# Order of the input projection's units, rotation angles computed directly, and channels stored by one operation in a hybrid S5 and attention trunk on one core

## The chip, the cores and the metric

The kernel runs on one core of a Trainium2 chip. TensorE (PE) does the matmuls, VectorE (DVE), ScalarE (ACT) and GpSimd (POOL) the element work, SyncE (SP) issues most DMAs. The metric is the device time of one execution in microseconds; of several executions the median is given.

## What is computed

The reference is one inference step of a two-layer trunk (layer 0: S5 mixer and sliding-window attention side by side; layer 1: a convolution module; a ConvGLU after each) for two groups of requests with the same weights: a prompt of 16 + 1024 tokens and 8 sampled sequences of 8 tokens. The change lies in the first mixer:

```python
h = rmsnorm(x, p['g_mix'][layer])
z = h @ p['w_in_mix'][idx]                        # 1024 -> 512 + 512 + 128 + 128
u = z[..., :D_SSM]                                # S5 channels
q = z[..., D_SSM:D_SSM + D_Q]                     # 8 heads of 64
k = z[..., D_SSM + D_Q:D_SSM + D_Q + D_KV]
v = z[..., D_SSM + D_Q + D_KV:]
ya, sr, si = s5_mixer(u, ...)     # a = exp(lambda dt), h_t = a h_(t-1) + B u_t, y = C h + d u, gelu, half-GLU
yb, nk, nv = swa_prompt(q, k, v, rel_bias, sink, w_rows)     # 128-wide window, softmax with a sink
x = x + concatenate([ya, yb]) @ p['w_out_mix'][idx]
```

The S5 scan runs over blocks of eight tokens: eight steps inside a block are one matrix, and from block to block a state is turned by the angle of 8 steps and shrunk. For this the kernel needs cos and sin of theta times 8 a and theta times 128 b (a up to 15, b up to 8), theta being the angle of one step for each of 32 groups with 64 states: the rotation tables `ta` and `tb`, whose products make the table `T`.

## The kernel before

Tokens are split into two streams, A with 528 columns and B with 576; activations stand channel by token, and stream B also has the sampled tokens. Matrices are kept in two parts, a rounded high part and the rest, and each product of a weight piece and an activation takes three matmuls (high by high, high by low, low by high), each in two halves of columns. A `Unit` is one block of 128 output channels with its eight k steps of 128 inputs (four in the output projection of one mixer half). Its weights come in pieces of 128 x 512 (four k steps), loaded by SP into four buffers (`raw`), rounded by ACT into `whi` (L210) and completed by DVE into `wlo` (L216). `mm` (L295) does a unit's matmuls (L315), then its epilogue `epi_...` empties the sum: `take` (L530) multiplies by the normalization's factor (Rk) into `kT`, `vst`, `qst`, while `epi_u` (L1403) stores the S5 channels `us` with eight operations, one for each of the eight places in a block of tokens, and sends them to DRAM (`uD`). Two units may run k step by k step together, as a `Pair`.

The units' list in `build` sets the order: before, (k, v) of A as a pair, q x 4, u x 4 of A, then u x 4, k, v, q x 4 of B, each named here as uA, uB and so on. Behind it follow the output projection's attention half on A (oA, six of its eight units), the gate of S5's A half (gluA), two more oA, and the S5 half on A (`yaA`), and so on.

Beside the units run generators in the background: after each k step `pump` (L325) advances every one by half its rate; a step issues a few operations on the engines. They are `take_x(B)` (x of stream B, its normalization), `rest`, the S5 preparation `s5_prep` (power tables, four pairs of tables: e, a table that makes psk, and f, a table of six operations that PE turns into psf, L843 to L848 and L879), S5's main loop (stage 1 is matmuls `xr`, `xi`, L923; stage 3 is `yps`, L965; eight pieces of each), attention on A in blocks (`attn_A`: scores L1232, `softmax_rows`, turn L1219, output L1246) and the gelus of S5's outputs (L1062). All of this is laid down at build time: each engine executes its own instructions in the order of their emission, and waits for other engines by semaphores. `s5_rot` (L697) builds the rotation tables on POOL with no step in between: some 130 operations on 128 x 16 raise a cosine and sine to the needed powers, some 50 more double them up to `ta` and `tb`, and then for each of four j six wide operations of 128 x 576 make the product table `tj`, which two DMAs send to DRAM (`tD`). The S5 loop starts (NU0) after eight u units.

## Time and profile before

| | us |
| --- | --- |
| median of 3 executions | 2436.97 |
| lowest, highest | 2433.14, 2439.76 |
| profiled execution | 2437.08 |
| span of the profile | 2435.3 |
| PE busy | 2339.9 (96%) |
| DVE busy | 1683.2 (69%) |
| ACT busy | 987.5 (41%) |
| POOL busy | 234.7 (10%) |

Busy times are over the whole span. In the page's 40 slices (61 us each) PE has 7, 6, 8, 9, 8 and 8 tenths in the first six, and 9 in all the others but the last, and POOL 5, 9, 4, 0 and 2 tenths in the first five: what is not PE at work stands in the first six slices, which are the loads and the input projection and the S5 and attention work beside it. The rows of the trace there are in the section behind the change.

### The profile page before, as it was taken

The page shows a single profiled execution, that of the slowest core. Times are in us where ns is not written, and L with a number is a line of the kernel's source. Part 1 is how long each engine was busy: PE and PEld are TensorE (multiplying, and loading weights), DVE is VectorE, ACT ScalarE, POOL GpSimd, SP SyncE. Part 2 cuts the span into 40 slices and gives each one's busy share as a digit, 9 for nine tenths or more (in the row PEclk, how much of TensorE's full clock was granted, in tenths as well). Part 3 has the DMA queues.
Part 4 walks back from the last instruction along what each step waited for, and adds up shares of the span by engine and source line. Part 5 has one row for each costly group of instructions (what it writes and reads, how often), then busy time and mean ns, then how long its engine had stood idle before and what let it go on. Part 6 is the DMA issues. An engine that isn't in the chain of part 4 may idle for free.

```text
span 2435.3 us, 46080 instructions
## 1 busy us (share of the span) xinstructions
PE 2339.9 (96%) x18180; PEld 2289.5 (94%) x18180; DVE 1683.2 (69%) x3135; ACT 987.5 (41%) x1890; POOL 234.7 (10%) x557
## 2 busy tenths in 40 slices
PE   7689889999999999999999999999999999999998
PEld 6577789889999999999999999999999999999998
DVE  6977666653778588888887568888888665444443
ACT  6233443553434343433326343343434534333343
POOL 5940200000000000100101000000000000000000
PEclk9889999998999999999999999999999999999999
DMA  7755744224333523223222432333332423222322
GB/s 207 227 143 159 221 137 151 76 68 116 88 95 92 165 65 101 83 79 87 79 82 84 122 126 75 102 88 98 89 97 83 130 75 113 79 87 77 89 83 69
DMA packets 459598, 260.86 MB, mean 107 GB/s; under 512 B 57451, under 2 KB 446727, under 8 KB 458198
## 3 DMA queue, kind: packets, MB, share of 16 engines
q1 hardware_dynamic: 456246, 253.08, 35.6%
q0 software_dynamic: 3136, 4.85, 0.7%
q8 instruction: 143, 2.34, 0.4%
q14 instruction: 73, 0.60, 0.1%
HBM read 225.59 MB, written 35.52 MB: 107 GB/s over the span
## 4 chain that ended last, share of the span: by engine, by line
PE 81%; DVE 7%; ACT 4%; DMA 2%; issue 2%; SPq 0%; POOL 0%; DVEq 0%; ACTq 0%; POOLq 0%
PE pu L315 78%; DVE wlo L216 1%; ACT whi L210 1%; PE tps L1219 1%; ACT P L1183 1%; PE sps L1232 1%; DVE mx L1176 0%; PE psum_s L367 0%; DMA m<-mD 0%; PE ops L1246 0%; DMA fstt<-in_state_ffn 0%; DMA raw<-in_w_out_mix 0%; ACT xB L1739 0%; DVE P L1236 0%; DMA xA<-xaD 0%
## 5 line engine op out<-in xcount | busy, mean ns | idle before, releaser
L216 DVE TENSOR_TENSOR wlo<-raw,whi 128x512 fp32r<-128x512 f32 x720 | 489.5, 683 | 516.5 <-ACT whi L210 512.1
L210 ACT CAST whi<-raw 128x512 fp32r<-128x512 f32 x720 | 434.5, 608 | 703.5 <-PE pu L315 640.3
L1674 DVE SCALAR_TENSOR_TENSOR xA<-gl,pt,xA 128x528 f32<-128x528 f32 x240 | 182.8, 763 | 3.8 <-ACT xA L1668 1.5
L1674 DVE SCALAR_TENSOR_TENSOR xB<-gl,pt,xB 128x512 f32<-128x512 f32 x240 | 179.0, 746 | 4.3 <-ACT xB L1668 2.9
L1493 ACT ACTIVATE cv<-cv 128x592 f32<-128x592 f32 (+2 forms) x88 | 58.9, 670 | 154.6 <-DVE cv L1492 154.5
L315 PE MATMUL pu<-a0h,whi 128*128 128x288 f32 (+3 forms) x428 | 92.2, 298 | 12.0 <-ACT G L1472 5.0
L1491 DVE SCALAR_TENSOR_TENSOR cv<-G,pt,cv 128x592 f32<-128x592 f32 (+2 forms) x88 | 70.1, 796 | 43.3 <-ACT cv L1490 42.4
L315 PE MATMUL pu<-a4h,whi 128*128 128x288 f32 (+3 forms) x420 | 89.2, 294 | 9.9 <-DVE xA L437 7.1
L315 PE MATMUL pu<-a1h,whi 128*128 128x288 f32 (+3 forms) x428 | 91.3, 295 | 0.0
L315 PE MATMUL pu<-a0l,whi 128*128 128x288 f32 (+3 forms) x428 | 90.4, 293 | 0.3 <-DVE a0l L218 0.3
L315 PE MATMUL pu<-a0h,wlo 128*128 128x288 f32 (+3 forms) x428 | 90.3, 293 | 0.0
L315 PE MATMUL pu<-a3h,whi 128*128 128x288 f32 (+3 forms) x428 | 90.3, 293 | 0.0
L315 PE MATMUL pu<-a2h,whi 128*128 128x288 f32 (+3 forms) x428 | 90.0, 292 | 0.0
L315 PE MATMUL pu<-a1h,wlo 128*128 128x288 f32 (+3 forms) x428 | 89.8, 292 | 0.0
L315 PE MATMUL pu<-a1l,whi 128*128 128x288 f32 (+3 forms) x428 | 89.5, 291 | 0.0
L315 PE MATMUL pu<-a2l,whi 128*128 128x288 f32 (+3 forms) x428 | 89.3, 290 | 0.0
L315 PE MATMUL pu<-a7h,whi 128*128 128x288 f32 (+3 forms) x420 | 89.2, 294 | 0.0
L315 PE MATMUL pu<-a2h,wlo 128*128 128x288 f32 (+3 forms) x428 | 89.1, 290 | 0.0
L315 PE MATMUL pu<-a3h,wlo 128*128 128x288 f32 (+3 forms) x428 | 88.9, 289 | 0.0
L315 PE MATMUL pu<-a5h,whi 128*128 128x288 f32 (+3 forms) x420 | 88.9, 293 | 0.0
L315 PE MATMUL pu<-a3l,whi 128*128 128x288 f32 (+3 forms) x428 | 88.9, 289 | 0.0
L315 PE MATMUL pu<-a6h,whi 128*128 128x288 f32 (+3 forms) x420 | 88.2, 292 | 0.0
(663 smaller groups left out, 6827.2 us busy)
## 6 DMA issues: line engine op xcount, KB each, us to landing
raw<-in_ffn_w_up SPq DMA_DIRECT2D x352, 256.0 KB, 2.9
raw<-in_ffn_w_down SPq DMA_DIRECT2D x128, 256.0 KB, 2.8
raw<-in_conv_w_pw SPq DMA_DIRECT2D x96, 256.0 KB, 2.7
raw<-in_ffn_w_down SPq DMA_DIRECT2D x64, 192.0 KB, 2.5
xbD<-xB SPq DMA_DIRECT2D x3, 2304.0 KB, 8.6
xB<-xbD SPq DMA_DIRECT2D x6, 1152.0 KB
raw<-in_w_in_mix SPq DMA_DIRECT2D x24, 256.0 KB, 4.3
xaD<-xA SPq DMA_DIRECT2D x2, 2112.0 KB
```

Of the source, the lines that this page charges most:

```text
L210: nc.scalar.copy(hi, src)
L216: nc.vector.tensor_tensor(lo, src, hi.bitcast(F32), op=OP.subtract)
L315: nc.tensor.matmul(ps[:, ch, :c], wt, xt[:, off + ch * c:off + (ch + 1) * c], start=(k == 0 and pi == 0), stop=(k == nk - 1 and pi == 2))
L1183: nc.scalar.activation(pt[:, h, :], pt[:, h, :], AF.Exp, bias=nm[:, h:h + 1], accum_out=sm[:, h:h + 1])
L1219: nc.tensor.transpose(v[:, h, :], pt[:, 4 * kv + h, ko:ko + m], self.ident[:nq, :nq])
L1232: nc.tensor.matmul(vs[kv][:, hh, :], q[hs, 2 * pr + hh, :], self.kT[hs, kc0:kc0 + nk], start=True, stop=True)
L1491: nc.vector.scalar_tensor_tensor(c, G[:, 1:1 + n], wc(1), c, op0=OP.mult, op1=OP.add)
L1493: self.chain(lambda: None, lambda: None, lambda: nc.scalar.activation(c, c, AF.Gelu_apprx_tanh))
L1674: V.scalar_tensor_tensor(acc, gl[:, i:i + npp], w(i), acc, op0=OP.mult, op1=OP.add)
```

## The change

The projection's units are put in another order: of A all (u0 and u1 as a pair, u2, u3, k, v, q x 4), then of B u x 4, and then k, v, q x 4. The rotation tables are computed directly: the angle of each multiple (its multipliers come with the mask as constants) is reduced to +-pi by POOL, and ACT takes its sine four times, in place of powers and doublings; the rotation is a background generator at rate 1, which waits 12 steps between the reduction and the sines, and then does the same wide operations, with a tile and a DMA for each of the two halves. The S5 channels are stored by one operation with a strided output and a DMA that reads the rows in reverse order. S5's main loop starts after six u units, its tables at rate 0.7, attention counts only the q of A, and the mask is loaded before x.

```diff
-NU0 = 8
+NU0 = 6
 WQ = 10
+WR = 12
 WA = 6
 WF2 = 8
 SP = 1
 K1 = 5
 K2 = 6
 VR = 3
-RP = 1.0
+RP = 0.7
...
+MAGIC = 12582912.0
+_C2 = math.floor((2 * math.pi - 6.28125) * 2 ** 21) / 2 ** 21
+TWOPI = (6.28125, _C2, 2 * math.pi - 6.28125 - _C2)
...
-        self.mask16 = pp.tile([P, 16], F32, name="mask16", tag="mask16")
+        mask = pp.tile([P, 41], F32, name="mask16", tag="mask16")
+        self.mask16, self.mult = mask[:, :16], mask[:, 16:]
+        nc.sync.dma_start(mask, a["c_mask16"])
...
-        nc.sync.dma_start(self.mask16, a["c_mask16"])
...
+        thh, thl = pl[:, 16, :], pl[:, 17, :]
+        V.tensor_scalar(thh, th, 12288.0, -12288.0, op0=OP.add, op1=OP.add)
+        V.tensor_tensor(thl, th, thh, op=OP.subtract)
...
-        def renorm(r, i):
-            G.tensor_tensor(q1, r, r, op=OP.mult)
-            G.tensor_tensor(q2, i, i, op=OP.mult)
-            G.tensor_tensor(q1, q1, q2, op=OP.add)
-            G.tensor_scalar(q1, q1, -0.5, 1.5, op0=OP.mult, op1=OP.add)
-            G.tensor_tensor(r, r, q1, op=OP.mult)
-            G.tensor_tensor(i, i, q1, op=OP.mult)
-
-        def square(dr, di, r, i):
-            G.tensor_tensor(q1, r, r, op=OP.mult)
-            G.tensor_tensor(q2, i, i, op=OP.mult)
-            G.tensor_tensor(q1, q1, q2, op=OP.subtract)
-            G.tensor_tensor(q2, r, i, op=OP.mult)
-            G.tensor_copy(dr, q1)
-            G.tensor_scalar(di, q2, 2.0, None, op0=OP.mult)
-            renorm(dr, di)
-
-        G.tensor_copy(e[:, 0, 0, :], cs)
-        G.tensor_copy(e[:, 0, 1, :], sn)
-        renorm(e[:, 0, 0, :], e[:, 0, 1, :])
-        for _ in range(3):
-            square(e[:, 0, 0, :], e[:, 0, 1, :], e[:, 0, 0, :], e[:, 0, 1, :])
-        for i in range(1, 8):
-            square(e[:, i, 0, :], e[:, i, 1, :], e[:, i - 1, 0, :], e[:, i - 1, 1, :])
-        w1 = tz[:, 0:256].rearrange("p (a b) -> p a b", a=16)
-        w2 = tz[:, 256:512].rearrange("p (a b) -> p a b", a=16)
         ta = pp.tile([P, 2, 16, 16], F32, name="ta", tag="ta")
         tb = pp.tile([P, 2, 16, 9], F32, name="tb", tag="tb")
-        for tt, base in ((ta, 0), (tb, 4)):
-            G.memset(tt[:, 0, :, 0:1], 1.0)
-            G.memset(tt[:, 1, :, 0:1], 0.0)
-            n = 1
-            lvl = 0
-            while n < tt.shape[3]:
-                m = min(n, tt.shape[3] - n)
-                bc = lambda ri: e[:, base + lvl, ri, :].unsqueeze(2).to_broadcast([P, 16, m])
-                self.cmul(G, tt[:, 0, :, n:n + m], tt[:, 1, :, n:n + m], tt[:, 0, :, 0:m], tt[:, 1, :, 0:m],
-                          bc(0), bc(1), w1[:, :, :m], w2[:, :, :m])
-                n += m
-                lvl += 1
+        sines = []
+        for tt, mult, off, m in ((ta, self.mult[:, 0:16], 0, 256), (tb, self.mult[:, 16:25], 512, 144)):
+            n = tt.shape[3]
+            x, h, k, w = (tz[:, off + m * i:off + m * i + m].rearrange("p (g a) -> p g a", g=16) for i in range(4))
+            mb = mult.unsqueeze(1).to_broadcast([P, 16, n])
+            th = lambda i: self.pl[:, i, :].unsqueeze(2).to_broadcast([P, 16, n])
+            G.tensor_tensor(k, th(4), mb, op=OP.mult)
+            G.tensor_scalar(k, k, 1.0 / (2 * math.pi), MAGIC, op0=OP.mult, op1=OP.add)
+            G.tensor_scalar(k, k, MAGIC, None, op0=OP.subtract)
+            G.tensor_tensor(x, th(16), mb, op=OP.mult)
+            for c in TWOPI[:2]:
+                G.tensor_scalar(h, k, -c, None, op0=OP.mult)
+                G.tensor_tensor(x, x, h, op=OP.add)
+            G.tensor_tensor(w, th(17), mb, op=OP.mult)
+            G.tensor_scalar(h, k, -TWOPI[2], None, op0=OP.mult)
+            G.tensor_tensor(w, w, h, op=OP.add)
+            G.tensor_tensor(x, x, w, op=OP.add)
+            G.tensor_scalar(x, x, 3.1415925, -3.1415925, op0=OP.min, op1=OP.max)
+            G.tensor_scalar(h, x, 0.0, -2.0, op0=OP.min, op1=OP.mult)
+            G.tensor_tensor(h, h, x, op=OP.add)
+            G.tensor_scalar(h, h, -1.0, math.pi / 2, op0=OP.mult, op1=OP.add)
+            sines += [(tt[:, 0], h), (tt[:, 1], x)]
+        for _ in range(WR):
+            yield
+        for out, x in sines:
+            nc.scalar.activation(out, x, AF.Sin)
         for j in range(4):
             g4 = slice(4 * j, 4 * j + 4)
-            tt = pp.tile([P, 2, 4, 9, 16], F32, name="tj", tag="tj")
             t1 = tz[:, 0:576].rearrange("p (g q b) -> p g q b", g=4, q=9)
             t2 = tz[:, 576:1152].rearrange("p (g q b) -> p g q b", g=4, q=9)
             f1 = lambda ri: ta[:, ri, g4, :].unsqueeze(2).to_broadcast([P, 4, 9, 16])
             f2 = lambda ri: tb[:, ri, g4, :].unsqueeze(3).to_broadcast([P, 4, 9, 16])
-            self.cmul(G, tt[:, 0], tt[:, 1], f1(0), f1(1), f2(0), f2(1), t1, t2)
             for ri in range(2):
-                nc.gpsimd.dma_start(self.dq(self.tD, ri, j, 132),
-                                    tt[:, ri].rearrange("p g q b -> p g (q b)")[:, :, 0:132])
+                G.tensor_tensor(t1, f1(0), f2(ri), op=OP.mult)
+                G.tensor_tensor(t2, f1(1), f2(1 - ri), op=OP.mult)
+                tt = pp.tile([P, 4, 9, 16], F32, name="tj", tag=f"tj{ri}")
+                G.tensor_tensor(tt, t1, t2, op=OP.add if ri else OP.subtract)
+                G.dma_start(self.dq(self.tD, ri, j, 132), tt.rearrange("p g q b -> p g (q b)")[:, :, 0:132])
...
-        rel = SA[:, 0:392]
+        rel = self.sacc.rearrange("p a b c -> p (a b c)")[:, 0:392]
...
-            self.nq += 1
+            self.nq += s is self.A
...
-            src = ps[:, :, :s.c].rearrange("p a (k s) -> p a k s", s=8)
-            R = self.R0[s.name].rearrange("p (a k s) -> p a k s", a=2, s=8)
-            for t in range(8):
-                dst = us[:, 7 - t, :].rearrange("p (a k) -> p a k", a=2)
-                nc.vector.tensor_tensor(dst, src[:, :, :, t], R[:, :, :, t], op=OP.mult)
-            nc.sync.dma_start(dap(self.uD, j * P * 8 * NK + s.col0 // 8, [[8 * NK, P], [NK, 8], [1, kk]]), us)
+            nc.vector.tensor_tensor(us.rearrange("p s (a k) -> p a k s", a=2),
+                                    ps[:, :, :s.c].rearrange("p a (k s) -> p a k s", s=8),
+                                    self.R0[s.name].rearrange("p (a k s) -> p a k s", a=2, s=8), op=OP.mult)
+            nc.sync.dma_start(dap(self.uD, (j * P * 8 + 7) * NK + s.col0 // 8, [[8 * NK, P], [-NK, 8], [1, kk]]), us)
...
-                self.s5_rot()
+                self.add_bg(self.s5_rot(), 1)
...
-        def in_units(s, h):
+        hA, hB = (lambda: self.hx["A"]), (lambda: self.hx["B"])
+        def channels(s, h):
             us = [Unit(self.wblock(win, 0, KT, j * P), h, s, self.epi_u(s, j)) for j in range(4)]
-            ks = [Unit(self.wblock(win, 0, KT, 1024), h, s, self.epi_k(s)),
-                  Unit(self.wblock(win, 0, KT, 1152), h, s, self.epi_v(s))]
-            return us, ks + [Unit(self.wblock_q(j), h, s, self.epi_q(s, j)) for j in range(4)]
-        uA, kA = in_units(A, lambda: self.hx["A"])
-        uB, kB = in_units(B, lambda: self.hx["B"])
-        items += [Pair(kA[0], kA[1])] + kA[2:] + uA + uB + kB
+            return [Pair(us[0], us[1])] + us[2:] if s is A else us
+
+        def heads(s, h):
+            return [Unit(self.wblock(win, 0, KT, 1024), h, s, self.epi_k(s)),
+                    Unit(self.wblock(win, 0, KT, 1152), h, s, self.epi_v(s))] + [
+                        Unit(self.wblock_q(j), h, s, self.epi_q(s, j)) for j in range(4)]
+        items += channels(A, hA) + heads(A, hA) + channels(B, hB) + heads(B, hB)
```

Three places show how the operations stand. On ACT, behind the activations of stream B (y6h, y7h are their rounded parts), in front of S5's first tables; before:

```order
L813 COPY h_1069<-psh 128x256
L212 ACTIVATE y6h<-xB,pt 128x576
L212 ACTIVATE y7h<-xB,pt 128x576
L833 COPY bd<-bb 64x8x16 x2
L210 CAST whi<-raw 128x512
L833 COPY bd<-bb 64x8x16 x2
L210 CAST whi<-raw 128x512
```

and now:

```order
L217 ACTIVATE y7h<-xB,pt 128x576
L782 COPY a_871<-apw 128x32
L215 CAST whi<-raw 128x512 x2
L802 COPY h_957<-psh 128x256
L735 ACTIVATE ta<-tz 128x256 x2
L735 ACTIVATE tb<-tz 128x144 x2
L822 COPY bd<-bb 64x8x16 x2
```

The four sine operations stand in front of the first copies of bd, behind h; before there are none, and POOL had nothing to wait for there.

On DVE, around the last of the four f tables (ff, L843 to L848 before, L832 to L837 now). Before, it stands behind the first us of A:

```order
L216 TENSOR_TENSOR wlo<-raw,whi 128x512
L868 MEMSET kz 128x112
L871 SCALAR_TENSOR_TENSOR kz<-mask_115,pt,kz 128x16
L216 TENSOR_TENSOR wlo<-raw,whi 128x512
L1413 TENSOR_TENSOR us<-pu,Rk 128x66 x8
L843 TENSOR_TENSOR ff<-bb,apw 128x512
L844 TENSOR_TENSOR y_1552<-bb,apw 128x512
L845 TENSOR_TENSOR ff<-ff,y_1552 128x512
L846 TENSOR_TENSOR ff<-bb,apw 128x512
L847 TENSOR_TENSOR y_1552<-bb,apw 128x512
L848 TENSOR_TENSOR ff<-ff,y_1552 128x512
L216 TENSOR_TENSOR wlo<-raw,whi 128x512
```

and now behind the last q of A (L535 is `take`):

```order
L857 MEMSET kz 128x112
L860 SCALAR_TENSOR_TENSOR kz<-mask_115,pt,kz 128x16
L535 TENSOR_TENSOR qst<-pu,Rk 128x528
L221 TENSOR_TENSOR wlo<-raw,whi 128x512 x2
L535 TENSOR_TENSOR qst<-pu,Rk 128x528
L832 TENSOR_TENSOR ff<-bb,apw 128x512
L833 TENSOR_TENSOR y_1584<-bb,apw 128x512
L834 TENSOR_TENSOR ff<-ff,y_1584 128x512
L835 TENSOR_TENSOR ff<-bb,apw 128x512
L836 TENSOR_TENSOR y_1584<-bb,apw 128x512
L837 TENSOR_TENSOR ff<-ff,y_1584 128x512
L221 TENSOR_TENSOR wlo<-raw,whi 128x512
```

The last table stands behind ten units of the new order, where before it stood behind seven.

On PE, at the end of the projections (y7 is the last k step of the last unit, a4 the first of an output unit). Before:

```order
L315 MATMUL pu<-y7h,whi 128x288 x2
L315 MATMUL pu<-y7l,whi 128x288 x2
L315 MATMUL pu<-y7h,wlo 128x288 x2
L315 MATMUL pu<-a4h,whi 128x264 x2
L315 MATMUL pu<-a4l,whi 128x264 x2
L315 MATMUL pu<-a4h,wlo 128x264 x2
L923 MATMUL xr<-u,xf 64x138 x4
L923 MATMUL xi<-u,xf 64x138 x4
```

and now:

```order
L320 MATMUL pu<-y7h,whi 128x288 x2
L320 MATMUL pu<-y7l,whi 128x288 x2
L320 MATMUL pu<-y7h,wlo 128x288 x2
L1221 MATMUL sps<-kT,xB 128x256 x8
L1235 MATMUL ops<-xB,vA 64x512 x4
L1030 MATMUL sps<-ident,hs 128x128
L1031 MATMUL sps<-ident,hf 16x128
L1030 MATMUL sps<-ident,hs 128x128
L1031 MATMUL sps<-ident,hf 16x128
L1208 MATMUL tps<-ident,xA 128x128 x16
L1235 MATMUL ops<-xB,vA 64x512 x4
L320 MATMUL pu<-a4h,whi 128x264 x2
```

The scores of the last block (sps), the turns and outputs (tps, ops) and S5's last states (hs, hf) now stand between the last projection unit and the first output unit, where before nothing stood; S5's stage 1, which before stood after the first k step of the output unit, is gone from there.

## Rows read from the trace of the kernel before

**Rows 1.** Stretches: length; busy (count) of PE, PEld, DVE, ACT, POOL; clock; DMA; GB/s.

```profile
49.50:122.30 72.80, 49.12 (x373) 44.70 (x373) 70.06 (x124) 23.96 (x54) 67.71 (x119) 0.80 0.66 205
122.30:155.30 33.00, 28.56 (x182) 26.55 (x183) 21.61 (x56) 10.80 (x45) 23.77 (x21) 0.74 0.66 154
155.30:274.60 119.30, 108.33 (x818) 91.78 (x817) 87.54 (x231) 46.34 (x138) 15.58 (x22) 0.96 0.61 164
274.60:335.20 60.60, 49.53 (x382) 46.70 (x381) 37.42 (x77) 29.84 (x54) 18.81 (x33) 0.92 0.61 168
335.20:2435.30 2100.10, 2069.73 (x16203) 2049.04 (x16203) 1436.17 (x2541) 846.41 (x1532) 85.58 (x275) 0.99 0.32 95
```

**Rows 2.** Waits of PE, 49.5 to 274.6 us: total, times, longest.

```profile
PE psf L879 <- DVE xA L1236: 9.1, 1, 9.1
...
PE tps L1219 <- DVE xA L1192: 3.5, 3, 1.6
```

**Rows 3.** Timeline of DVE: start, duration, line, operation, shapes, idle before.

```profile
61.17 0.69 DVE L530 TENSOR_TENSOR qst<-pu,Rk 128x528 f32<-128x528 f32 x1
...
72.19 1.04 DVE L843 TENSOR_TENSOR ff<-bb,apw 128x512 f32<-128x512 f32 x1
...
77.53 0.78 DVE L823 TENSOR_TENSOR ee<-ct,apw 128x576 f32<-128x576 f32 x1
...
109.64 0.68 DVE L216 TENSOR_TENSOR wlo<-raw,whi 128x512 fp32r<-128x512 f32 x1
110.24 1.55 DVE L1413 TENSOR_TENSOR us<-pu,Rk 128x66 f32<-128x66 f32 x8
111.72 1.31 DVE L843 TENSOR_TENSOR ff<-bb,apw 128x512 f32<-128x512 f32 x1
...
122.27 1.64 DVE L216 TENSOR_TENSOR wlo<-raw,whi 128x512 fp32r<-128x512 f32 x1
```

**Rows 4.** Timeline of POOL: the rotation's operations.

```profile
90.76 0.40 POOL L589 TENSOR_TENSOR tz<-ta,e 128x128 f32<-128x128 f32 x1
...
111.00 1.16 POOL L588 TENSOR_TENSOR tz<-ta,tb 128x576 f32<-128x576 f32 x1
...
137.29 1.18 POOL L589 TENSOR_TENSOR tz<-ta,tb 128x576 f32<-128x576 f32 x1
```

**Rows 5.** Timeline of PE after the projections' end.

```profile
275.43 0.69 PE L923 MATMUL xr<-u,xf 128*64 128x138 f32 x8
...
278.07 1.10 PE L965 MATMUL yps<-u,m 128*128 128x138 f32 x8
...
288.51 0.48 PE L315 MATMUL pu<-a4h,whi 128*128 128x264 f32 x2 [3.87 <-DVE xA L437]
...
307.26 0.78 PE L315 MATMUL pu<-a4h,whi 128*128 128x264 f32 x2 [3.21 <-DVE xA L437]
```

**Rows 6.** Waits of PE, 274.6 to 335.2 us.

```profile
PE pu L315 <- DVE xA L437: 7.1, 2, 3.9
PE pu L315 <- ACT th L1421: 3.1, 3, 2.2
```

**Rows 7.** Timeline of DVE in one attention block.

```profile
222.94 1.29 DVE L1236 SCALAR_TENSOR_TENSOR xA<-sps,xB 128x512 f32<-128x512 f32 x2
224.26 2.29 DVE L1176 TENSOR_REDUCE mx<-xA 128x8 f32<-128x2048 f32 x1
...
245.14 2.19 DVE L1192 TENSOR_SCALAR xA<-xA,smx 128x256 f32<-128x256 f32 x8
```

**Rows 8.** Timeline of ACT in an attention block, and a table load.

```profile
226.78 0.51 ACT L1183 ACTIVATE xA<-xA,nm 128x256 f32<-128x256 f32 x1 [4.24 <-DVE nm L1178]
...
230.73 0.19 ACT L1184 ACTIVATE es<-es 128x8 f32<-128x8 f32 x1
...
249.91 1.09 ACT L1220 COPY xB<-tps 128x512 f32<-128x512 f32 x2
...
263.52 1.28 ACT L1062 ACT_TABLE_LOAD   x1
```

More of the change, by code (lines that the diff above doesn't have):

```diff
@@ L659, in s5_prep1 @@
         V.tensor_tensor(den, lr, dt, op=OP.mult)
-        magic = 12582912.0
-        V.tensor_scalar(nn, th, 1.0 / (2 * math.pi), magic, op0=OP.mult, op1=OP.add)
-        V.tensor_scalar(nn, nn, magic, None, op0=OP.subtract)
+        V.tensor_scalar(nn, th, 1.0 / (2 * math.pi), MAGIC, op0=OP.mult, op1=OP.add)
+        V.tensor_scalar(nn, nn, MAGIC, None, op0=OP.subtract)
         yield
-        c1 = 6.28125
-        c2 = math.floor((2 * math.pi - c1) * 2 ** 21) / 2 ** 21
-        c3 = 2 * math.pi - c1 - c2
-        for cc in (c1, c2, c3):
+        for cc in TWOPI:
             V.scalar_tensor_tensor(th, nn, -cc, th, op0=OP.mult, op1=OP.add)
```

12 lines of the change are left out of this document (4 added, 8 removed).

## The prediction

> **What bounds the kernel now.** I first read the table of stretches [rows 1]. From 335.20 us on PE is busy for 2069.73 of 2100.10 us at a granted clock of 0.99, and the change touches nothing there, so all that it can move lies in the first 335 us. I cut these at five places of the program: 49.5, where the weights' first delay ends; 122.3, where the last S5 table has been built; 155.3, where PE reaches the eighth k step (y7) of uB0, the eleventh unit; 274.6, the end of the projections; 335.2, the first unit of yaA. From 49.5 to 122.3 DVE is busy for 70.06 of 72.80 us while PE has 49.12 at a clock of 0.80: DVE bounds that stretch, and PE waits for its tables, weights and sums. From 155.3 to 274.6 PE has 108.33 of 119.30 us: PE bounds it, with waits between. From 274.6 to 335.2 PE has 49.53 of 60.60.
>
> Then the waits of PE up to 274.6 [rows 2]: the longest is one of 9.1 us in front of the transposition of the last table (psf), whose last releaser is an operation of DVE, and attention's turn waits 3.5 us for DVE's scaling in three places. That agrees with DVE as the bound. The timeline of DVE [rows 3] shows what stretches it: an f table of six operations takes from 72.19 to 77.53, 5.34 us, but the last one takes from 111.72 to 122.27, 10.55 us. The timeline of POOL [rows 4] shows the reason beside it: its wide rotation operations begin at 111.00. Six of them lie in that table, so each costs DVE (10.55 - 5.34) / 6 = 0.87 us.
>
> **Part 1, the first stretch (49.5 to y7 of uB0).** The new order puts u0 to u3 of A, then k, v and the four q of A in front of uB0, which are the same ten units in another order; the rotation now starts in the background, and its 24 wide operations come while tables are still being built. In the order of DVE the last f table now follows the last q of A, when 10.9 units have been summed, so that its end is the place which before was reached at 155.3. I count DVE's list up to it from 122.3.
>
> Six more weight pieces (wlo) come ahead of it, at a step of 0.60 us from one row's start to the next [rows 3]: 3.7 with the gaps. The epilogues: before, one `us` of eight operations, 1.55 us, and four takes of 0.69; now two `us` operations and six takes. The single strided `us` isn't in the trace; its bounds are 0.69 (a plain operation of 528 columns) and 1.55 (the eight together), and I take 1.0, nearer to the plain one, because the tables' own strided first operation takes 1.04. That is 6.1 for 4.3, about +1.7. Ten small operations on powers, which stood just before 49.5, move behind it: +1.2. Sum +6.6. The contention that was in the last table goes: -5.2.
>
> The 24 wide operations then all fall beside tables. POOL's own duration undisturbed is 1.18 us, beside DVE 1.16 at first [rows 4]. At 0.87 each DVE loses 21; if only the table operations collide, some 0.63 of DVE's work there, 13. I take 16.5, between the two, since weights read SBUF in the same form as tables and epilogues don't. So the table ends at 122.3 + 6.6 - 5.2 + 16.5 = 140.2 (137 to 145), in place of 155.3: **15.1 us gained**. The gain comes from the 33 us between 122.3 and 155.3, in which PE had 28.56 us of work at 0.74 of the clock: work that now stands beside the tables.
>
> The range reduction adds 32 POOL operations of 256 and 144 columns. None is in the trace; between 0.40 us at 128 columns and 1.18 at 576 [rows 4] they cost about 0.62 and 0.43, 17 us of POOL, in place of some 180 small ones. I cost them at nothing, since they lie before 49.5, where DVE waits for weights; without that cover their 16 two-input operations cost up to 8. The tiles `tj` split in two remove POOL's waits for its own DMA, behind which no other engine's work stood. The sine operations (four on ACT) come behind the copy of psh and hold nothing that PE needs for over 2 us. The mask's load ahead of x costs the start 0.5 us (0 to 1).
>
> **Part 2, from y7 of uB0 to the projections' end.** 119.3 us before. PE gets work that stood elsewhere: one more stage 1 of S5 (two groups, the first of 0.69, which overlap: 1.1), three stage 3 (1.10 for the first half [rows 5] and as much for the second, with hand-overs 6.8 together) and the scores of blocks 0 and 1 (4). It loses block 4 (6.1, by its number of matmuls) and one output (1.9), which now lie behind. That is +3.9. Of PE's 3.5 us of waits for DVE's scaling [rows 2] the part beside the late POOL operations goes, about 1.9. So about +2, and the projections end at 140.2 + 121.3 = 261.5, for 274.6. As attention starts 32 k steps later and S5 earlier, both engines get more even work; I give it no price.
>
> **Part 3, from there to yaA.** 60.6 us before. What goes: S5's matmuls, stage 1 and three stage 3, 7.9 by the same durations and some 2 more as a part of them ran at the lower clock (0.92 granted in this stretch [rows 1]), 9.9; of the 7.1 us of waits for DVE's sums [rows 6] all but 1, since the first, 3.87 at 288.51 [rows 5], stands behind the reload of xA, which is now issued before the output units, and the second, 3.21 at 307.26, behind S5's last states, which now come earlier: -6.1; of the 3.1 behind `th` 2.7, as the gelus of B come earlier. Sum -18.7.
>
> What is added is the tail of attention. In PE's new order nothing stands between block 4's scores and the output units but its own turn and output, so the chain of one block lies bare [rows 7, 8]; pieces without a row there are estimates from their columns: scores 1.5; the scaled sum of four, 2 x 1.29 = 2.5; the maximum 2.29; two small ones and their hand-over 0.5; eight exponentials, from 226.78 to 230.73, 4.0; their sums' reciprocal 0.6; the scaling 2.2; the turn with four copies of which two take 1.09, 2.9; gelu and table loads of 1.28 on ACT ahead of these copies, 2.5; output 1.3; copy and cast 1.2; a hand-over of some 0.2 at three places. That is 22.2. Behind so long a pause PE starts at the lower clock, as at 307.26, where a pair takes 0.78 for 0.48 [rows 5] after 3.21 us; I take 2 for it. So 60.6 - 18.7 + 24.2 = 66.1, and yaA starts at 327.6, for 335.2: -7.6. With the mask -7.1, and with PE's slightly shorter waits for gB behind it some -8. The profiled execution took 2437.08 us (span 2435.3), the median of the three runs is 2436.97; so they stand 0.1 apart and I predict **2429**.
>
> **A rule against it.** The trace prices one wide POOL operation at 0.87 us of DVE, less than its own 1.16. The Trainium skill ("SBUF — State Buffer", section "SBUF: two separate sides") says that GpSimd and a DVE operation with two SBUF inputs share a port pair as an exclusive lock, held for the whole instruction, the other fully blocked. By that the six operations would have cost their full duration, 7; measured are 5.2, so the trace agrees in kind and less in size. By the rule the 24 would cost 28 and the program come to 2441; by the rows it is 2429. What the rule does here is the rival R1 below, with its own price from rows.
>
> **The rivals.** *R1, slower:* each of the 24 wide operations blocks DVE for all of its 1.18 us, 28 for 16.5, and half of the range reduction, up to 8, falls where DVE works. The first stretch then ends at 152 to 160 and the program at 2441 to 2449, say 2445. It decides from 24.5 us of contention upwards for a loss at all (16.5 + 8). For it speaks that the operations now meet a DVE without a gap; against it 5.2 for six. *R2, no change:* the tail of attention takes 8 us more than I count, because ACT's gelus and their table loads (four more, at 1.28) stand in front of the exponentials and the copies; what PE won before is waited for again, 2437. For it speaks that the chain crosses three engines that are not idle; against it that in before the block's chain went through next to gelus without such delay. *R3, faster:* contention is small (8), since POOL's operations mostly meet DVE operations that read PSUM or weights, and of the 11 us of waits in the second stretch half go, as S5 and attention no longer stand in front of each other: 2429 - 8.5 - 5.5 = 2415. For it speaks that neither engine is full there (DVE 87.54 of 119.30), against it that attention's chain crosses three engines in any order. *That the change doesn't do what it says* I leave out, as the orders of both show every move.
>
> **How the numbers follow.** What three runs can tell from no change is about 0.3%, 7.3 us. Forecast 0.45 (2420 to 2438, so somewhat over half of it is faster), R1 0.20, R2 0.16, R3 0.19. Faster: 0.45 x 0.57 + 0.19 = 0.45. Same: 0.45 x 0.40 + most of R2 and a fifth of R1 = 0.33. Slower: four fifths of R1 and the edges of the forecast and of R2, 0.22. The range 2410 to 2446 leaves out the ends of R1 and R3; the bounds of `us`, mask and contention lie within.
>
> **What would show it.** Right: DVE's last f table ends near 140 with the wide POOL operations beside it at up to 2 us, PE passes y7 of uB0 at about the same time, the projections end near 261, a pause of some 20 us of PE follows behind the last scores, with exponentials and copies in it, and yaA starts near 327. Wrong in step 1: the table ends after 150, or PE waits for something other than DVE. Wrong in step 3: PE's pause is below 15 or above 28 us, or output units run within it. Wrong as a whole: a difference behind yaA of more than 3 us, since I say that nothing there moves.

## The result, and the profile after

The changed kernel takes 2461.19 us (median of four runs, 2458.16 to 2464.56) against 2435.46 of the kernel before: a ratio of 1.0104, interval 1.0082 to 1.0125. It is slower by 25.7 us, where I had predicted 2429. Its profiled execution took 2459.4 us (span 2457.6).

The stretches of the changed kernel, cut at the same places of the program as [rows 1], in the same columns (y7 of uB0, the end of the projections, the first output unit, yaA):

```profile
49.50:150.00 100.50, 67.29 (x495) 62.74 (x496) 95.27 (x122) 25.74 (x55) 42.23 (x37) 0.78 0.64 184
150.00:284.80 134.80, 115.12 (x906) 99.84 (x904) 88.93 (x238) 52.49 (x169) 20.24 (x35) 0.92 0.68 172
284.80:317.00 32.20, 13.79 (x53) 6.92 (x53) 13.14 (x31) 18.09 (x38) 8.03 (x15) 0.63 0.30 71
317.00:359.10 42.10, 37.41 (x289) 36.40 (x289) 24.60 (x38) 19.27 (x29) 0.00 (x0) 0.96 0.39 122
359.10:2457.60 2098.50, 2069.20 (x16203) 2049.57 (x16203) 1436.71 (x2541) 846.74 (x1531) 85.64 (x275) 0.99 0.32 95
```

| place | before | forecast | after |
| --- | --- | --- | --- |
| y7 of uB0 | 155.6 | 140.2 | 150.0 |
| from there to the end of the projections | 119.0 | 121.3 | 134.8 |
| from there to yaA | 60.6 | 66.1 | 74.3 |
| yaA | 335.2 | 327.6 | 359.1 |

All three stretches came out longer than forecast, by 9.8, 13.5 and 8.2 us. Behind yaA the kernel takes 2098.5 us, before it took 2100.1: nothing moved there.

**First stretch.** The timeline of DVE in the changed kernel, in the first f table:

```profile
92.59 3.81 DVE L832 TENSOR_TENSOR ff<-bb,apw 128x512 f32<-128x512 f32 x1
96.33 2.21 DVE L833 TENSOR_TENSOR y<-bb,apw 128x512 f32<-128x512 f32 x1
98.58 3.05 DVE L834 TENSOR_TENSOR ff<-ff,y 128x512 f32<-128x512 f32 x1
101.55 2.25 DVE L835 TENSOR_TENSOR ff<-bb,apw 128x512 f32<-128x512 f32 x1
103.71 3.46 DVE L836 TENSOR_TENSOR y<-bb,apw 128x512 f32<-128x512 f32 x1
107.20 1.78 DVE L837 TENSOR_TENSOR ff<-ff,y 128x512 f32<-128x512 f32 x1
...
109.50 0.70 DVE L535 TENSOR_TENSOR kT<-pu,Rk 128x528 f32<-128x528 f32 x1
```

It takes from 92.59 to 108.90, 16.3 us, where [rows 3] show 5.34 for a table alone and 10.55 for the worst of before. The timeline of POOL beside it:

```profile
93.22 1.18 POOL L743 TENSOR_TENSOR tz<-ta,tb 128x576 f32<-128x576 f32 x1
94.35 1.17 POOL L744 TENSOR_TENSOR tz<-ta,tb 128x576 f32<-128x576 f32 x1
95.60 2.07 POOL L746 TENSOR_TENSOR tj<-tz 128x576 f32<-128x576 f32 x1
...
98.78 1.17 POOL L743 TENSOR_TENSOR tz<-ta,tb 128x576 f32<-128x576 f32 x1
```

POOL's products (tz) keep the 1.16 to 1.18 us of [rows 4], while the DVE operations beside them take 1.8 to 3.8: here POOL works back to back and DVE stands behind it each time. Only POOL's third operation of each half (tj) is lengthened, to 1.43 to 2.07 us; in e16, where DVE stands idle beside it, the timeline of POOL has

```profile
165.49 1.40 POOL L748 TENSOR_TENSOR tj<-tz 128x576 f32<-128x576 f32 x1
```

The later f tables, with POOL quiet, take 5.5, 6.1 and 6.6 us. The single `us` takes 1.13 to 1.29 us, and at 528 columns the next operation starts 0.97 us behind its start; I had taken 1.0.

**Second stretch.** The waits of PE from 150 to 284.8 (total, times, longest):

```profile
PE tps L1208 <- ACT xs L924: 6.8, 2, 5.0
PE xr L912 <- DMA xf<-xfD: 6.1, 1, 6.1
PE yps L954 <- ACT xA L1237: 2.2, 1, 2.2
PE vps L1146 <- DVE vst L535: 2.1, 1, 2.1
```

Its waits sum to 19.3 us, before to 10.9. The one that grew most is that of `xr` for the table xf from DRAM; in the waits of before, from 155.6 to 274.6, it is

```profile
PE xr L923 <- DMA xf<-xfD: 0.6, 1, 0.6
```

PE's busy time is 115.12 us there instead of 108.03, at a granted clock of 0.92 instead of 0.96.

**Third stretch.** The tail of attention in the timeline of PE:

```profile
284.72 1.14 PE L1221 MATMUL sps<-kT,xB 64*128 64x256 f32 x8
288.98 2.56 PE L1221 MATMUL sps<-kT,xB 64*128 64x256 f32 x8 [3.12 <-ACT xB L1209]
...
310.18 3.56 PE L1208 MATMUL tps<-ident,xA 128*128 128x128 f32 x16 [11.30 <-DVE xA L1181]
...
316.98 0.39 PE L320 MATMUL pu<-a4h,whi 128*128 128x264 f32 x1 [1.37 <-ACT a4h L215]
```

and in the timeline of ACT:

```profile
286.62 1.16 ACT L1051 ACTIVATE gt<-yrd 128x528 f32<-128x528 f32 x1 [3.60 <-DMA yrd<-yD]
...
298.45 0.51 ACT L1172 ACTIVATE xA<-xA,nm 128x256 f32<-128x256 f32 x1 [7.22 <-DVE nm L1167]
...
303.07 1.28 ACT L1051 ACT_TABLE_LOAD   x1
304.37 1.15 ACT L1051 ACTIVATE gt<-yrd 128x528 f32<-128x528 f32 x1
...
306.61 1.23 ACT L1051 ACTIVATE gt<-yrd 128x576 f32<-128x576 f32 x1
```

and of DVE:

```profile
306.20 0.71 DVE L221 TENSOR_TENSOR a3l<-gt,a3h 128x528 fp32r<-128x528 f32 x1 [7.59 <-ACT a3h L215]
308.57 0.76 DVE L221 TENSOR_TENSOR y4l<-gt,y4h 128x576 fp32r<-128x576 f32 x1 [1.65 <-ACT y4h L215]
...
309.68 2.19 DVE L1181 TENSOR_SCALAR xA<-xA,smx 128x256 f32<-128x256 f32 x8
```

From the last scores to the first output unit it is 32.3 us. The second half of the scores starts at 288.98 because ACT holds the copies of an earlier turn behind a gelu, which had itself waited 3.60 us for its DMA; the exponentials end at 302.5, but DVE's scaling comes only at 309.68, since a table load, two gelus and their roundings (303.07 to 308.5) stand in ACT's order ahead of two operations of DVE (306.20 and 308.57) that stand ahead of the scaling. The links of the chain that have rows take what was forecast (the scaled sum 2.47, the maximum 2.29, the exponentials 4.0, the scaling 2.19 us). What stands in between was put at 2.5 us, and the gap behind the exponentials alone is 7.2.

### The profile page after: what moved, and what is told of

It is laid out like the page before. It is cut to its first block, busy times and chain, and to the rows that moved or that the text cites. A ratio compares the mean times of both kernels' runs of the same rounds, so it can differ in the third digit from the quotient of the medians.

```text
span 2457.6 us, 45896 instructions
## 1 busy us (share of the span) xinstructions
PE 2338.2 (95%) x18180; PEld 2286.9 (93%) x18180; DVE 1695.2 (69%) x3081; ACT 995.5 (41%) x1898; POOL 182.4 (7%) x409
## 4 chain that ended last, share of the span: by engine, by line
PE 82%; DVE 9%; ACT 3%; DMA 3%; issue 2%; SPq 1%; POOL 0%; DVEq 0%; ACTq 0%; POOLq 0%
PE pu L320 79%; DVE wlo L221 1%; DMA raw<-in_w_in_mix 1%; PE tps L1208 1%; DVE mx L1165 1%; ACT whi L215 1%; ACT P L1172 1%; DMA yrd<-yD 0%; ACT xA L1172 0%; PE psum_s L372 0%; DMA xbD<-xB 0%; DMA uD<-us 0%; ACT gt L1051 0%; PE yps L954 0%; PE sps L1221 0%
## 5 line engine op out<-in xcount | busy, mean ns | idle before, releaser
L320 PEld LDWEIGHTS pu<-a0h,whi 128*128 128x128 f32 x428 | 68.2, 192 | 24.9 <-issue 8.1
```

The lines of the kernel that those rows point to most:

```text
L320: nc.tensor.matmul(ps[:, ch, :c], wt, xt[:, off + ch * c:off + (ch + 1) * c], start=(k == 0 and pi == 0), stop=(k == nk - 1 and pi == 2))
```

## The experiments

The places of all runs, from the starts of PE's operations in each trace, in us: y7 of uB0; from there to the end of the projections; from there to the first output unit; from there to yaA. The ratio is to the kernel before on the same chip, with its 95% interval. The places are those of the one execution that was traced, and the stretch behind yaA, in which the runs do the same work, took from 2091.5 us (e1) to 2102.1 (e13); so a place and a median need not agree. The traced execution of e1 lay 10.6 us under its median, that of e5 7.2 over it.

| run | y7 | projections | pause | to yaA | median | ratio |
| --- | --- | --- | --- | --- | --- | --- |
| before | 155.6 | 119.0 | 0 | 60.6 | 2435.5 | |
| after | 150.0 | 134.6 | 32.4 | 42.1 | 2461.2 | 1.0104 (1.0082 to 1.0125) |
| e1 | 138.6 | 135.3 | 32.3 | 42.2 | 2452.3 | 1.0052 (1.0033 to 1.0072) |
| e2 | 140.9 | 135.3 | 34.2 | 41.9 | 2451.0 | 1.0053 (1.0036 to 1.0069) |
| e3 | 149.3 | 144.9 | 0 | 52.2 | 2446.5 | 1.0040 (1.0026 to 1.0054) |
| e4 | 145.4 | 139.3 | 32.6 | 41.6 | 2460.4 | 1.0089 (1.0064 to 1.0115) |
| e5 | 135.2 | 133.4 | 34.4 | 41.5 | 2439.4 | 1.0014 (1.0002 to 1.0026) |
| e6 | 166.2 | 117.2 | 0 | 62.2 | 2445.5 | 1.0043 (1.0030 to 1.0057) |
| e7 | 139.6 | 142.6 | 0 | 53.0 | 2436.3 | 0.9991 (0.9982 to 1.0000) |
| e8 | 166.1 | 115.8 | 0 | 62.2 | 2443.2 | 1.0023 (1.0013 to 1.0033) |
| e9 | 139.2 | 145.7 | 0 | 55.3 | 2437.8 | 1.0003 (0.9987 to 1.0019) |
| e10 | 128.0 | 130.1 | 32.6 | 42.0 | 2432.8 (one run) | |
| e11 | 145.1 | 129.4 | 0 | 62.2 | 2438.4 | 1.0007 (0.9994 to 1.0021) |
| e12 | 148.7 | 125.1 | 38.0 | 42.3 | 2455.7 | 1.0075 (1.0050 to 1.0100) |
| e13 | 121.5 | 129.6 | 34.0 | 41.8 | 2431.9 | 0.9975 (0.9959 to 0.9990) |
| e14 | 120.9 | 157.3 | 3.5 | 52.7 | 2433.9 | 0.9985 (0.9971 to 1.0000) |
| e15 | 121.0 | 150.0 | 0 | 62.7 | 2432.4 | 0.9981 (0.9966 to 0.9996) |
| e16 | 122.1 | 161.0 | 31.3 | 42.2 | 2462.5 | 1.0118 (1.0095 to 1.0141) |
| e17 | 123.3 | 144.6 | 18.9 | 45.0 | 2429.9 | 0.9984 (0.9971 to 0.9997) |

### The price of the wide POOL operations (e1, e5, e10)

e1 leaves them out:

```diff
-                G.tensor_tensor(t1, f1(0), f2(ri), op=OP.mult)
-                G.tensor_tensor(t2, f1(1), f2(1 - ri), op=OP.mult)
                 tt = pp.tile([P, 4, 9, 16], F32, name="tj", tag=f"tj{ri}")
-                G.tensor_tensor(tt, t1, t2, op=OP.add if ri else OP.subtract)
+                nc.scalar.copy(tt, f1(ri))
```

> The changed kernel, with the 24 wide rotation operations on POOL left out (the table T is then not the product that the reference needs; one ACT copy of 128x576 stands for each of the eight halves). Theory (POOL's wide operations hold DVE for their whole 1.17 us each, 28 us, in the first stretch): the last f table ends 20 to 28 us earlier than at 150.8 us, an f table takes about 5.3 us everywhere, and the program takes 2437 to 2443 us. Rival (the first stretch is long because of the longer list of weights and epilogues, or because of the loads): less than 6 us go, 2455 us or more.

y7 came at 138.6, 11 us earlier, and the program at 2452.3, between the two. The f tables took 5.4 to 6.6 us, but the substitute had a fault of its own: ACT's copies wait for the DMAs of the two tiles `tj` (22.2 us in five waits), and PE stood 18.8 us for a copy of bd that came behind them on ACT. So e5 put memsets on POOL instead, whose waits hold no one else:

```diff
+                G.memset(tt, 0.5)
```

> The changed kernel, with the 24 wide rotation operations on POOL left out and one POOL memset of 128x576 for each of the eight halves in their place, which reads nothing from SBUF (the table T is then not the product). No engine but POOL waits for the tiles' DMA now, unlike the run with ACT copies, where ACT's queue stood behind it for 18.5 us. Theory (the wide operations cost the first stretch 28 us): the last f table ends between 121 and 127 us, 24 to 30 before the changed kernel's 150.8, and the program takes 2430 to 2440 us. Rival (without them PE's own work or the loads hold the stretch at about the 139 us of the run with ACT copies): 2448 us or more.

The DVE operations of the same f table in e5:

```profile
76.56 1.04 DVE L830 TENSOR_TENSOR ff<-bb,apw 128x512 f32<-128x512 f32 x1
77.52 1.07 DVE L831 TENSOR_TENSOR y<-bb,apw 128x512 f32<-128x512 f32 x1
78.63 0.69 DVE L832 TENSOR_TENSOR ff<-ff,y 128x512 f32<-128x512 f32 x1
...
82.47 0.70 DVE L535 TENSOR_TENSOR kT<-pu,Rk 128x528 f32<-128x528 f32 x1
```

From the second iteration of the normalization's root to the take of kT (82.47 here, 109.50 after) DVE executes the same operations in both. The iteration starts in e5 and in the changed kernel at

```profile
66.00 0.17 DVE L361 TENSOR_TENSOR w<-y,v 128x5 f32<-128x5 f32 x1
```

```profile
64.46 1.05 DVE L361 TENSOR_TENSOR w<-y,v 128x5 f32<-128x5 f32 x1
```

So it is 16.5 us in e5 and 45.0 in the changed kernel: 28.5 us for 24 wide operations, 1.19 each. POOL's own time for them, undisturbed, is some 30 us (16 products of 1.17 and eight third operations of 1.40, 1.25 on average), so DVE loses nearly as much. POOL's memsets of e5 lengthen no operation of DVE there. Theory and number hold on DVE. The program took 2439.4, as expected, but y7 came at 135.2 in the trace, and the last f table ended at 135.9 for the 121 to 127 that I had expected, for a reason further down the stretch. The waits of ACT and of SP's queue in e5:

```profile
ACT whi L215 <- DMA raw<-in_w_in_mix: 27.8, 5, 11.7
```

```profile
SPq L1092 <- DMA xbD<-xB: 11.5, 1, 11.5
```

Weights came late because SP, in order, waited 11.5 us in front of the load of attention's bias, which goes into the area of xB and waits for xB's store. In e10 that load is on POOL's queue:

```diff
-        self.load_bias(SB[:, 0:2048].rearrange("p (h k) -> p h k", h=8))
+        self.load_bias(SB[:, 0:2048].rearrange("p (h k) -> p h k", h=8), nc.gpsimd)
```

> The run with memsets in place of the wide rotation operations (the table T is not the product), with the bias load on POOL's queue. Theory: the last f table ends at 122 to 128 us instead of 135.9, since DVE's own list has no more than that, and the wait of ACT for a weight load (11.7 us) is under 3. Rival (bandwidth): 133 us or more.

The last f table ended at 126.7 us, y7 came at 128.0, and ACT waited 1.6 us for weights in place of 27.8. So my list of DVE (122.3 + 6.6 - 5.2 = 123.7) was right within 3 us in this one execution, and the contention was the mis-sized term of part 1.

### The same work on DVE (e2, e7, e9)

```diff
-                G.tensor_tensor(t1, f1(0), f2(ri), op=OP.mult)
+                V.tensor_tensor(t1, f1(0), f2(ri), op=OP.mult)
...
                 G.dma_start(self.dq(self.tD, ri, j, 132), tt.rearrange("p g q b -> p g (q b)")[:, :, 0:132])
+                yield
```

So do the other two operations of a half.

> The changed kernel with the same 24 wide operations on DVE in place of POOL, one step of the background for each half (three operations). Theory (a POOL operation blocks DVE for 1.17 us, more than the operation would cost DVE itself, 0.76 as the tables' e operations): the last f table ends about 10 us earlier and the program takes 2449 to 2454 us. Rival (the two engines share and the sum of DVE's own work is the bound): DVE has 18 us more to do, 2465 us or more.

y7 came 9 us earlier (140.9) and the program at 2451.0, as the theory said: the 24 operations cost DVE less when DVE does them. e7 adds attention's rate of e3 (below), e9 also the queue of e10:

```diff
-RT = 1.6
+RT = 2.4
```

> The changed kernel with the wide rotation operations on DVE and attention's rate at 2.4. Theory (the two costs lie in different stretches and add): some 9 and 14 us less than the changed kernel, 2434 to 2441 us. Rival (what one gives is taken back by the other, since DVE is the engine of both): 2446 us or more.

> The changed kernel with the wide rotation operations on DVE, attention's rate at 2.4, and the load of attention's bias issued by POOL's queue in place of SP's (it waits for the store of xB, and on SP the weights queue behind it). Theory (without the contention the loads of weights are what ends last: in the run with memsets ACT waited 11.7 us for one of them and SP 11.5 us in front of the bias): y7 of uB0 is passed some 8 us earlier than in the same kernel with SP's queue (139.6 us), and the program takes 2425 to 2431 us. Rival (the loads are late by their own bandwidth, not by their order): 2434 us or more.

e7's two gains did add (2436.3, no more than the kernel before). e9 missed (2437.8): y7 at 139.2, as in e7. ACT's waits for weights are not among its longest in e9, where DVE has 18 us more to do, and the queue was worth nothing there.

### The parts alone (e4, e6)

e4 is the changed kernel with `s5_rot` and `epi_u` of before; e6 is the kernel before with the new `s5_rot` (and its constants and early mask):

```diff
-                self.add_bg(self.s5_rot(), 1)
+                self.s5_rot()
```

```diff
-                self.s5_rot()
+                self.add_bg(self.s5_rot(), 1)
```

> The changed kernel with the rotation and the storing of channels as before: only the order of the units, the S5 start and rates, and the early mask are changed. Theory (the order has the attention tail of 32 us and the later S5 work; the old rotation's wide operations start about 110 us and fall half on a full DVE): 2445 to 2455 us, with a last f table at about 140 us and the same tail. Rival (the loss comes from the rotation alone): 2430 to 2438 us.

> The kernel before with the new rotation alone (angles by range reduction and sines, in the background, early mask); the order of units, the start of S5 and the storing of channels as before. Theory (24 wide POOL operations on a full DVE cost 28 us, where before some 5 fell on a full DVE and the rest beside waits): the last f table ends 15 to 24 us later than at 122.3, and the program takes 2448 to 2460 us. Rival (the new rotation is as good as the old, and the loss is the order's): 2433 to 2440 us.

e4 missed: with the old rotation the new order takes 2460.4, as much as the whole change, though y7 came 4.6 us earlier; the stretch behind was as much longer. e6's verdict is the theory's, its size under it: the last f table ended 18 us later, as expected, but y7 came 10.6 us later and the program took 2445.5. The waits of PE in e6 up to there:

```profile
PE pu L320 <- DVE qst L535: 15.0, 2, 14.4
PE psf L868 <- DVE ff L834: 11.1, 3, 7.2
```

The first f tables took 11.9 and 9.3 us. So the two costs are no sum: the order, with S5's early start and the new rates (e4 has all three), costs as much as the whole change, the rotation alone 0.43%, and on top of the new order the new rotation with the single store adds nothing.

### The tail of attention and S5's start (e3, e12)

e3 is the edit of RT above, alone; e12 is this one alone:

```diff
-NU0 = 6
+NU0 = 8
```

> The changed kernel with attention's background rate at 2.4 for 1.6, so that by the order the last output of attention stands in the ninth of the ten units behind uA and none behind the projections. Theory (the 32 us between the projections' end and the first output unit are the bare chain of attention's last block): this pause shrinks to under 8 us, the projections end some 5 us later, and the program takes 2437 to 2445 us. Rival (ACT and DVE are what is full there, and the chain only moves): PE waits as much within the projections, 2455 us or more.

e3 took 2446.5, 1.5 us over the theory's range: the pause of 32 us is gone, but the projections took 10.3 us longer and the output units 10.1. The two stretches, in the columns of [rows 1]:

```profile
149.30:294.20 144.90, 121.70 (x952) 102.51 (x951) 99.36 (x259) 59.96 (x196) 18.95 (x33) 0.94 0.61 157
294.20:346.40 52.20, 40.51 (x295) 39.30 (x294) 26.97 (x46) 23.66 (x35) 9.39 (x18) 0.90 0.54 151
```

By this 12 of the 32 us are gained, and 20 come back. Of these some 10 are PE's own work, which had stood in the pause (PE is busy for 162.2 us in the two stretches, after for 152.3), and some 10 are waits at other places.

> The changed kernel, S5's main loop started after eight u units as before, in place of six. Theory (of the 15 us that the stretch from y7 of uB0 to the end of the projections is longer than before, 8 are S5's, which starts before its tables have come back from DRAM, 6.15 us at one place): this wait goes, but S5's last pieces then stand behind the projections, in the attention tail: 2453 to 2462 us. Rival (the earlier start of S5 costs nothing and helps the tail): 2465 us or more.

e12 took 2455.7, as expected: the projections 9.5 us shorter, the tail 5.6 longer. But its interval overlaps that of the changed kernel, and the wait of `xr` for xf from DRAM did not go, as I had said it would (5.6 us, for 6.1). The projections in e12:

```profile
148.70:273.80 125.10, 104.75 (x816) 91.99 (x814) 79.92 (x209) 46.67 (x154) 11.43 (x19) 0.92 0.66 166
```

PE has 90 matmuls less there than after, and its busy time is 10.4 us shorter; its waits are as long as after, 20 us. So what left this stretch is S5's work, not waiting.

### Rotation behind the tables (e8, e11, e13, e16)

e8 gates the wide operations in the kernel before on five u units at build time:

```diff
+        while self.nu < 5:
+            yield
         for j in range(4):
```

> The kernel before, its order kept, with the channels stored by one operation and the new rotation, whose wide operations start only when five u units are done, so behind the last f table, a half for each step of the background; S5's main loop waits for them. Theory (a wide POOL operation costs DVE 1.17 us, which costs the program nothing where DVE has idle time): the last table loses the 5.2 us of contention, the wide operations fall at 150 to 190 us, where DVE was idle for a fourth of the time: 2424 to 2433 us. Rival (in that stretch attention's chain goes through DVE and each delay is PE's): 2436 to 2445 us.

It missed (2443.2), since it did not do what was meant: the wide operations ran at 69.5 to 111.7, much as in e6. That its time lies in the rival's range says nothing about the rival. What is emitted later isn't later on an engine that has nothing to do before it: POOL ran ahead. e11, the kernel before with the same new rotation and single store, gates the sines, for which POOL waits, on the tables' end:

```diff
+        while not self.tabs:
+            yield
         for out, x in sines:
             nc.scalar.activation(out, x, AF.Sin)
...
             yield from self.s5_prep()
+            self.tabs = 1
+            while not self.rotdone:
+                yield
```

> The kernel before with the channels stored by one operation and the new rotation, whose sines on ACT are issued behind the last f table, so that POOL's wide operations, which wait for them, cannot run earlier (emission alone did not delay them, POOL had run ahead). Theory (a wide operation costs DVE 1.17 us, and costs the program nothing where DVE isn't full): the last f table ends at 117 to 119 us, the wide operations run from some 140 to 185 us, and the program takes 2426 to 2434 us. Rival (attention's chain on DVE is what PE waits for there): 2437 us or more.

The last f table ended at 111.3, before at 122.3, y7 came 10.5 us earlier, the wide operations ran at 121 to 161, and the projections ended at 274.4, before at 274.6: all of it was given back, and the rival's 2437 or more is met (2438.4). From y7 to there PE waits 20.2 us, before 11.0. In e11, from 49.5 to 160, PE waited for attention's scaling on DVE:

```profile
PE tps L1212 <- DVE xA L1185: 13.0, 6, 2.8
```

[rows 2] had 3.5 for that, up to 274.6; e11 has no more of these waits up to 274.4. That the wide operations lie under this chain is seen in the timeline; that they alone make these waits was not tried. e13 has the same gate in the changed kernel, with the edits of e10 (the bias on POOL's queue) and e12 (`NU0 = 8`):

> The changed kernel with its sines issued behind the last f table (so that the wide POOL operations start behind it), the bias load on POOL's queue, and S5's start after eight u units; attention's rate as in the changed kernel. Theory (the wide operations cost what they cost only where DVE is full; what they take from the first stretch isn't given back as in the before order, where S5 and attention shared the stretch behind it): y7 of uB0 at 127 to 131 us, the stretch behind it 125 to 132 us, the tail of attention 32 to 38 us, 2436 to 2444 us. Rival (it is given back, as in the run e11): the stretch behind y7 is longer by as much as the first is shorter, 2450 us or more.

e13 took 2431.9, faster than both kernels (than the kernel before by 0.25%) and than its forecast. Its first two stretches, in the columns of [rows 1]:

```profile
49.50:121.50 72.00, 61.81 (x495) 57.87 (x496) 66.54 (x122) 24.68 (x51) 4.15 (x7) 0.93 0.82 231
121.50:251.10 129.60, 106.50 (x816) 93.02 (x814) 98.40 (x220) 47.37 (x157) 49.52 (x52) 0.91 0.73 178
```

y7 at 121.5 is 28.5 us earlier than in the changed kernel, as much as the whole contention; the stretch behind is 5 us shorter, and the tail (34.0) is still there. e16 has the gate alone, with S5's start at six:

> The changed kernel with one edit only: its sines are issued behind the last f table, and S5's main loop, which starts after six u units as in the changed kernel, waits for the rotation to be issued; the bias load stays on SP's queue, attention's rate is as in the changed kernel. Theory (the contention is 28 us of the first stretch, of which the weights behind SP's bias load keep 7 when it goes alone, as the memsets showed): y7 of uB0 at 128 to 136 us, and the stretch behind it as in the changed kernel, some 135 us and a tail of 32, so 2440 to 2448 us. Rival (the gain of e13 came from S5's later start or the queue): 2452 us or more.

y7 at 122.1, and still 2462.5 in all, in the rival's range: the stretch behind took 161.0 us instead of 134.6. S5's first operation of DVE on the rotation table in e16, and the wait of PE that follows from it:

```profile
168.77 0.43 DVE L924 TENSOR_TENSOR X<-xr,T 128x260 f32<-128x260 f32 x1 [21.54 <-DMA T<-tD]
```

```profile
169.84 2.00 PE L1225 MATMUL sps<-kT,xB 64*128 64x144 f32 x8 [16.86 <-ACT xs L928]
```

S5 starts early, its first DVE operation waits 21.54 us for T, and ACT's copy, the attention scores and PE stand behind it in order. So the rotation has to be early for a start at six and late for the tables. With the start at eight the late one costs the stretch behind y7 4.5 us (129.6 in e13, 125.1 in e12), where it saves 27 ahead of it. The queue of the bias wasn't needed for y7 (122.1 with SP's); the late rotation with a start at eight and SP's queue was not run.

### Tail and late rotation together (e14, e15, e17)

e14, e15 and e17 are e13 with RT at 2.0, 2.4 (and `NU0 = 7`) and 1.8:

```diff
-RT = 1.6
+RT = 2.0
```

> As e13, with attention's rate at 2.0, by which its last output stands in the last projection unit. Theory (the tail goes, the stretch before it takes 8 to 15 us more): 2422 to 2432 us, faster than the kernel before. Rival (attention's chain on ACT and DVE costs as much inside the projections as behind them): 2436 us or more.

> As e14, with attention's rate at 2.4 and S5's start after seven u units. Theory: within 4 us of e14, since neither tail nor S5 stands behind the projections in either. Rival (the denser attention meets the late rotation on DVE): 6 us or more over e14.

> As e13, with attention's rate at 1.8, by which the last scores stand at the start of the last projection unit and only the last turn and output behind it. Theory (the tail costs the more the later its scores are, and the projections pay only where the chain is dense): the tail falls to under 18 us, the projections end some 5 us later: 2420 to 2428 us. Rival (what leaves the tail comes back within the projections, as in e14): 2430 us or more.

None beat e13 by more than the intervals. In e14 the pause fell to 3.5 us and the projections grew by 27.7, the output units by 10.9. Its projections in the columns of [rows 1]:

```profile
120.90:278.20 157.30, 123.85 (x864) 102.08 (x862) 107.62 (x237) 57.46 (x184) 50.30 (x52) 0.86 0.60 152
```

Of the 27.7 us 17.4 are PE's busy time (48 matmuls more, at a granted clock of 0.86 for 0.91) and 10.4 are waits. From y7 to yaA PE waits 43.0 us, in e13 39.8, and is busy 4.9 us longer. e14's 2433.9 lies between its theory and its rival; e15 lies within 2 us of e14, as expected; e17 (2429.9, 0.9984) missed by little in time, but its projections took 15 us longer for the 5 expected, with a pause of 18.9. The rival's mechanism is what the places show: whatever leaves the tail comes back in the stretches beside it. The lowest ratio is e13's, 0.9975.

## Why the prediction was wrong

**What bounds the kernel** was read right. DVE was the bound of the first stretch, and its list without contention (123.7 by my sum) ended at 122.3 in e13, 122.8 in e16 and 126.7 in e10.

**The contention term** of part 1 failed: 28.5 us for the forecast 16.5. I took 0.87 us an operation from the one table of before and then a discount for DVE operations that were thought not to collide. The 0.87 came from a place where DVE's operations had also held POOL up, as POOL's next rows in the kernel before show, behind that of 111.00 in [rows 4]:

```profile
112.12 1.94 POOL L589 TENSOR_TENSOR tz<-ta,tb 128x576 f32<-128x576 f32 x1
114.14 2.06 POOL L590 TENSOR_TENSOR tj<-tz 128x576 f32<-128x576 f32 x1
```

There both engines lost: the six operations took POOL 10.7 us for the 7.5 of undisturbed ones, and DVE lost 5.2. In the changed kernel POOL's products ran undisturbed, its third operations lost some 3 us in all, and DVE lost 28.5. In e5 against after the price is 1.19 us an operation, nearly POOL's whole duration (1.25), and even operations of 128 x 5 columns stood for 1.05 to 3.06 us. It is the price of R1, whose stretch (152) was missed by only 2 us; its second part, the range reduction on a working DVE, did not come: e13 and e16 have the same reduction, and their list ends no later than my sum, which puts it at nothing. The rule quoted there (the Trainium skill, "SBUF — State Buffer", section "SBUF: two separate sides") fits these rows better than my reading of the row of before did: the trace agrees, with 28.5 us for 24 operations against the 28 that I had worked out by it.

**Part 2** failed most: +15.6 for +2. I counted PE's matmuls (+3.9) and took the waits of before less 1.9. PE's busy time rose by 7.1 (at a granted clock of 0.92 for 0.96), and the waits rose by 8.4 in place of falling; 5.5 of that is the wait of `xr` for xf. S5's early pieces and attention's chain now share this stretch. I had written that I give this no price; that was the error.

**Part 3**: the sum of the pieces that go was right (42.1 us from the first output unit to yaA, by my sum 60.6 - 18.7 = 41.9), but in part by luck: PE's work fell by 12.1 us (49.53 to 37.41) for the 9.9 that I had counted, and 4.7 us of waits were left for some 2.3. The tail was 32.4 for 24.2, mainly for the reason that R2 had named, gelus and a table load of ACT in the chain, at its price of 8 us; the scaled sum also came some 2 us behind the scores, as DVE had S5's last states and a take to do first. The `us` did what it was put at; the mask's early load was not measured alone.

**The verdict.** No single rival gave the result: R1's price and R2's price came together (11.8 + 8), with the 13.5 of part 2 on top, and I had let each stand alone. With R1 and R2 together, 2449 would have been forecast, still 12 us short.

**What stays open:** how the 8.4 us of waits in part 2 divide between attention and S5. By the last releaser 5.5 are S5's wait for xf, but e12, with S5's later start, has that wait too and 20 us of waits in all, so a later start alone does not take them away. Open is also why a denser attention (e3, e14) costs within the projections and output units so much of what it saves in the pause: part of it is PE's work that has only moved, part is waits at other places, and which of DVE and ACT causes these was not tried.

## What to carry to other kernels

Beside a full DVE these wide POOL operations, which read SBUF, cost DVE nearly their whole duration, and memsets cost it nothing; put such work where DVE has idle time, or on DVE itself if that is shorter (18 us for 28 here). A gain on one stretch can be lost where the next consumer starts too early for it: in this kernel the late rotation with S5's start at eight (and the bias on POOL's queue) was worth 29 us, the start alone 5.5, which the intervals don't separate from nothing, and the late rotation alone nothing. And where a chain loses its cover, count everything that stands in the order of its engines between its links, not its links alone.

## What was not expected of the hardware

How long a DVE operation stands beside POOL can have little to do with its own size. A 128 x 5 operation, 0.17 us in e5, took 3.06 us in the changed kernel, until POOL's two products were done, and these were not lengthened:

```profile
68.58 3.06 DVE L364 TENSOR_SCALAR rB<-y 128x5 f32<-128x5 f32 x1
```

```profile
69.31 1.18 POOL L743 TENSOR_TENSOR tz<-ta,tb 128x576 f32<-128x576 f32 x1
70.43 1.18 POOL L744 TENSOR_TENSOR tz<-ta,tb 128x576 f32<-128x576 f32 x1
```

What held it in the 0.73 us ahead of the first product isn't shown. And a table load on ACT (1.28 us at 303.07) is followed by the gelu at 304.37 at once: of a further cost of a switch the trace shows nothing.
